# Grouped Ln and Exp in the mixer's front, and weight blocks' lower halves by accumulating DMAs

## The chip, the cores and the metric

The kernel runs on one core of one Trainium2 chip. The metric is the time of one execution in device microseconds (us); the time of the kernel before is the median of three runs. Engines have the profile's names: PE (TensorE's matmuls) and PEld (its weight loads, which overlap them), DVE (VectorE), ACT (ScalarE), POOL (GpSimd) and SP (SyncE, which here only issues DMAs).

## The reference

One decoder layer on 512 tokens of width 1024, with 16 learned tokens put in front (528 rows). After an RMSNorm, one matrix gives all projections. Half of the width goes through RWKV-7 time mixing (8 heads of 64), the other half through an mLSTM (4 heads). Both are joined by `w_out`; then come an RMSNorm and a mixture of 32 SwiGLU experts, of which each token uses two; a last RMSNorm ends it. What the change touches is in the RWKV part:

```python
w_log = -jax.nn.softplus(-(w0 + jnp.tanh(xw @ w_la) @ w_lb)) - 0.5
kk = (k * k_k).reshape(B, L, H, N)
kk = kk / jnp.maximum(jnp.sqrt(jnp.sum(kk * kk, axis=-1, keepdims=True)), 1e-12)
decay = jnp.exp(-jnp.exp(heads(w_log)))
def step(S, inp):
    r_t, d_t, k_t, v_t, a_t, b_t = inp
    Sa = jnp.einsum('bhvk,bhk->bhv', S, a_t)
    S = S * d_t[:, :, None, :] + Sa[..., None] * b_t[:, :, None, :] + v_t[..., None] * k_t[:, :, None, :]
    return S, jnp.einsum('bhvk,bhk->bhv', S, r_t)
y = ((y - mu) * lax.rsqrt(var + LNX_EPS)).reshape(B, L, RWKV_WIDTH)
```

## The kernel before, in words

**Two stages.** The front (projections, RWKV, mLSTM, `w_out`, router) comes first; then the experts, in 16 pairs. A pair's weights are 12 DMAs of 1 MB, so the experts' stage reads some 200 MB. `fetch` (L1731) issues them on SP in order as soon as there is room in SBUF, the first from the planner's mark "var" on (`prefetch`, L1956), most of them when the projections have given their inputs' room back.

**Projections.** `PLAN` (L34) lists 28 blocks of 128 columns: K, R, V for RWKV (four each), v, q, o for the mLSTM, L, M, e, a, b for the low-rank parts. Activations and weights are each split into a rounded upper half and a lower half, and a block is 8 steps (`proj_k`, L600) of (upper, upper), (upper, lower), (lower, upper) on two spans of 264 columns: 48 matmuls, of which the fifth is the first that reads the weights' lower half. `projections` (L1018) prepares the next block after the second step of the current one (L1042) and loads a further one from HBM after the fourth (L1044). `split_block` (L516) makes the halves: ACT casts the raw block to the upper half, and DVE or POOL subtracts that from the raw block. `prepare` (L681) picks the engine: POOL from the mark "P3" to the mark "chain" (and later for q), else DVE. Upper and lower halves have three pairs of places, in the tiles arR and arQ.

**RWKV.** `decays` (L788) makes, per group j of two heads, the decays' running sums and three Exps. `norms` (L826) makes the keys' norms: Square on ACT, a matmul that sums over a head, a max on DVE, then Ln and Exp(-0.5 x) on ACT. `heads` and `products` (L846, L912) make what the 64-token chunks need and set "P0" to "P3". Then `inverse` (L1382) inverts 64 triangular matrices by 31 dependent steps of small DVE operations (`interleaved`, L1345), starting from identity matrices that a DMA of `eye` writes (tile XL, L1386); `inverse0` (L1367) does the same on POOL for the first 16 tokens (XL0, L1374). `chain` (L1490) then walks the chunks, each waiting on the one before. After it `variances` (L1561) makes the heads' variances, per quarter tb: Square, a matmul into one PSUM bank, Ln, and at the end Exp for all four. `outputs_a` (L1584) needs these ("var") and the gate `Gw` of `gate_a` (L1313), and gives what the `mixer` (L1866) multiplies by `w_out`.

**What sets the order.** PE's and SP's instructions run in the order in which they are emitted. `Weave.run` (L422) picks the next generator by rank and by a model of time, `Clock` (L181), in which POOL's `tensor_tensor` costs 2.1 ns per element of a row (L264), a DMA its bytes at 360 GB/s and 2 us more (L244, L290), and a change between Ln and Exp/Tanh 1.28 us (L274). That POOL and DVE hinder each other is not in it. The order on DVE, ACT and POOL is made by the framework's scheduler, from priorities (which follow the order of emission; `tc.high_priority` raises them) and its own estimate of when an instruction's inputs are there. All of the front's instructions are recorded at one line, L308, by a helper.

Of the kernel before, what the change touches and what calls it, by code (L numbers as in the profile page):

```python
# [9 lines left out]
F32 = mybir.dt.float32  # L10
# [7 lines left out]
L = 528  # L18
# [340 lines left out]
class Weave:  # L359
# [21 lines left out]
    def until(self, *names):  # L381
        while any(n not in self.marks for n in names):
            yield self.clock.t + 0.2
# [60 lines left out]
def layer(ctx, tc, a, out, dbg=None, stop=None):  # L444
# [27 lines left out]
    if dbg is not None and "track" in dbg:  # L472
        dbg["track"](A, B)

    def dump(name, ap):
        if dbg is not None and name in dbg:
            Y.dma_start(out=dbg[name], in_=ap)
# [5 lines left out]
    def chunks(t):  # L483

        return t[:, NM:].rearrange("p (c t) -> p c t", t=64)
# [10 lines left out]
    def c(name, i=0, n=1):  # L496
        return cv[:, CV[name][0] + i:CV[name][0] + i + n]
# [9 lines left out]

    lead, rest, small, wide = range(0, 4), range(4, 8), range(4, 6), range(6, 8)


    def load_block(i):
        raw = A.get([128, 1024], name="raw")
        Y.dma_start(out=raw, in_=a["wb"][i])
        return raw

    def split_block(raw, hi_by=S, lo_by=V, among=None):  # L516
        hi, lo = A.get([128, 1024], F32R, "whi", among), A.get([128, 1024], F32R, "wlo", among)
        if hi_by is S:
            S.copy(hi, raw)
        else:  # L520
            gcopy(hi, raw)
        lo_by.tensor_tensor(lo, raw, hi.bitcast(F32), op=OP.subtract)
        A.put(raw)
        return hi, lo, (hi, lo)

# [262 lines left out]
    def decays():  # L788

        yield from until("hwa")  # L790
        for j in range(4):
# [22 lines left out]
            D65 = Dt[:, 17:].rearrange("p (c t) -> p c t", t=65)  # L814
            G.memset(Dt[:, 0:1], 1.0)
            G.memset(D65[:, :, 0:1], 1.0)
            S.activation(Dt[:, 1:17], sg[:, :NM], AF.Exp, scale=-DEC)
            S.activation(D65[:, :, 1:], chunks(sg), AF.Exp, scale=-DEC)
            S.activation(sg, sg, AF.Exp, scale=DEC)
            gcopy(DT[:, j, 0:1], Dt[:, 16:17])  # L820
            gcopy(DT[:, j, 1:9], D65[:, :, 64])
            gates_of[j] = sg, al, Dt, D65
# [2 lines left out]

    def norms():  # L826

        for j in range(4):
            yield from until(f"k{j}")
            yield from W.units(A, 1)  # L830
            sq = A.get([128, L], name="sq")
            S.activation(sq, kx[j], AF.Square, scale=c("k_k", j))
            yield from need(sq)
            pn = yield from bank(2, "pn", rest)
            for h in range(2):
                P.matmul(pn[:, h, :264], m("bones"), sq[:, h * 264:h * 264 + 264], start=True, stop=True)
            V.tensor_scalar(halves(sq), pn[:, :, :264], 1e-24, None, op0=OP.max)
            B.put(pn)
            S.activation(sq, sq, AF.Ln)
            S.activation(sq, sq, AF.Exp, scale=-0.5)  # L840
            V.scalar_tensor_tensor(sq, kx[j], c("k_k", j), sq, op0=OP.mult, op1=OP.mult)
            nks[j] = sq
            yield
            W.mark(f"n{j}")

    def heads():  # L846

# [516 lines left out]
    VS, VU, Wt, SD = [], [], None, None  # L1364
    Btu = Bt.rearrange("p c j x -> p (c j) x")

    def inverse0():  # L1367
        yield from until("P3")
        NC0, NL0 = A.get([128, NM, 32], name="NC0"), A.get([128, NM, 32], name="NL0")
        XL0 = A.get([128, 32, NM], name="XL0")  # L1370
        tm0 = [A.get([128, 64], name="tm0")]
        G.memset(NC0, 0.0)
        gcopy(NC0[:, :, 0:4].rearrange("p t j -> p j t"), Bt0)
        Y.dma_start(out=XL0, in_=a["eye"][None, :, 0:NM].to_broadcast([128, 32, NM]))  # L1374
        V.transpose(NL0.rearrange("p a b -> p (a b)"), NC0.rearrange("p a b -> p (a b)"))
        yield from interleaved(G, XL0, lambda s: NL0[:, s + 1:, s], NM, tm0, 99)
        V.transpose(NC0, XL0.rearrange("p r t -> p t r"))
        gcopy(X0, NC0[:, :, 0:4].rearrange("p t j -> p j t"))
        A.put(NC0, NL0, XL0, *tm0)
        W.mark("X0")  # L1380

    def inverse():  # L1382
        yield from until("P3")
        NL = A.get([128, 32, 32], name="NL")
        XL = A.get([128, 32, 32], name="XL")
        Y.dma_start(out=XL, in_=a["eye"][None].to_broadcast([128, 32, 32]))  # L1386
        tmps = [A.get([128, 256], name="tmp") for _ in range(2)]
        V.transpose(NL.rearrange("p a b -> p (a b)"), NCt.rearrange("p a b -> p (a b)"))
        yield from interleaved(V, XL, lambda s: NL[:, s + 1:, s], 32, tmps, 8)
# [171 lines left out]
    def variances():  # L1561

        f = "p j x -> p (j x)"
        yield from until("chain")
        for tb in range(4):
            W.add(1, variance(tb, yT[tb].rearrange(f), sqs[tb].rearrange(f)))
        yield from until(*(f"var{tb}" for tb in range(4)))
        for sq in sqs:
            S.activation(sq, sq, AF.Exp, scale=-0.5)
        W.mark("var")  # L1570

    def variance(tb, y, sq):
        S.activation(sq, y, AF.Square)
        yield from need(sq)
        pm_ = yield from bank(1, "pm", every)
        P.matmul(pm_, m("bones"), sq, start=True, stop=True)
        S.activation(sq, pm_, AF.Ln, scale=1.0 / 64, bias=m("eps")[:, 1:2])
        yield
        B.put(pm_)
        W.mark(f"var{tb}")  # L1580

    ya = {}

# [379 lines left out]

    W.add(0, heads())
    W.add(0, chain())
    W.add(0.69, inverse0())
    W.add(0, decays())
    W.add(1, norms())
# [378 lines left out]
```

## Time and profile before

| | us |
|---|---|
| median of 3 runs | 905.73 |
| lowest and highest run | 905.42, 906.67 |
| the profiled execution's own time | 904.07 |
| its span, first to last instruction | 902.3 |

| engine | busy us | share |
|---|---|---|
| PE | 826.9 | 92% |
| PEld | 499.0 | 55% |
| DVE | 434.1 | 48% |
| ACT | 264.3 | 29% |
| POOL | 203.1 | 23% |

A share is an average over the whole span. The front and the experts' stage have different limits, so the rows further below are read by stretch. In a row of the timeline, instructions of the same kind that follow each other are merged: its second column is then the time from the first one's start to the last one's end. What stands in square brackets is idle time of the engine ahead of the row, and who ended it.

### The profile page before, as it was taken

To read this page: it belongs to the slowest core of one execution; us is meant where nothing else is said; L and a number is where in the kernel's file an instruction comes from. 1 tells how busy PE (TensorE), PEld (TensorE's weight loads), DVE (VectorE), ACT (ScalarE), POOL (GpSimd) and SP (SyncE) were. 2 spreads that over 40 slices of the span, in tenths; PEclk is the share of its full clock that TensorE was granted. 3 is DMA by queue.
4 is the path that set the end of the run, shared out by engine and by line. 5 is a ranking of instruction groups with operands and counts; after the bars stand their busy time and mean duration, and the time that the engine had idled before them with its cause. 6 is when DMAs were issued, how large, how long until landed. Compare 5 with 4: busy or idle time off the path is not lost. (4 is left out here: it accounts for less than half of the span.)

```text
span 902.3 us, 13658 instructions
## 1 busy us (share of the span) xinstructions
PE 826.9 (92%) x5487; PEld 499.0 (55%) x5488; DVE 434.1 (48%) x819; ACT 264.3 (29%) x505; POOL 203.1 (23%) x278
## 2 busy tenths in 40 slices
PE   7989697878899889999999999999999999999994
PEld 5878596777887767888343444433444423332331
DVE  7677757598746639437132333423333323331324
ACT  5755555634345584312110111001110101001102
POOL 5164625365543328220100000000000000000002
PEclk8988889988998899999999999999999999999998
DMA  6210111311300222989999999999999999999982
GB/s 238 71 42 7 47 63 55 83 34 38 102 25 2 74 84 72 386 329 348 376 406 393 419 420 420 420 420 420 420 420 420 420 421 420 420 419 422 421 349 97
DMA packets 45142, 235.60 MB, mean 261 GB/s; under 512 B 9906, under 2 KB 10290, under 8 KB 21008
## 3 DMA queue, kind: packets, MB, share of 16 engines
q1 hardware_dynamic: 42192, 228.58, 63.6%
q0 software_dynamic: 2160, 3.93, 1.1%
q10 hardware_dynamic: 720, 2.15, 0.6%
q8 instruction: 45, 0.74, 0.3%
q14 instruction: 25, 0.20, 0.1%
HBM read 234.38 MB, written 4.19 MB: 264 GB/s over the span
## 5 line engine op out<-in xcount | busy, mean ns | idle before, releaser
L308 PE MATMUL accs<-arS,arR 128*128 128x264 f32 (+2 forms) x1136 | 180.8, 311 | 8.3 <-DVE arS L308 3.5
L308 PEld LDWEIGHTS accs<-arS,arR 128*128 128x128 f32 (+1 forms) x1136 | 160.6, 199 | 22.4 <-issue 5.5
L308 PE MATMUL accs<-arF 64*64 64x192 f32 (+17 forms) x1361 | 112.6, 289 | 29.8 <-DVE arF L308 20.0
L2072 PE MATMUL accs<-arF 128*64 128x512 f32 x568 | 133.2, 599 | 6.2 <-DMA arF<-wgu 6.1
L2000 DVE TENSOR_TENSOR arF<-arF,accs 128x512 f32<-128x512 f32 x124 | 80.8, 683 | 100.4 <-PE accs L1998 98.9
L308 PEld LDWEIGHTS accs<-arF 64*64 64x64 f32 (+6 forms) x1346 | 83.1, 157 | 46.3 <-DVE arF L308 15.9
L308 POOL TENSOR_TENSOR arF<-arF 128x528 f32<-128x528 f32 (+13 forms) x97 | 89.9, 929 | 83.1 <-DVE arF L308 56.6
L1809 POOL DMA_INDIRECT arM<-hd,arF x15 | 15.1, 1008 | 372.8 <-DVE arF L1799 356.1
L308 DVE TENSOR_TENSOR arF<-arF 64x16 f32<-64x16 f32 (+31 forms) x170 | 90.2, 578 | 7.4 <-POOL arF L308 4.7
L2072 PEld LDWEIGHTS accs<-arF 128*64 128x64 f32 x568 | 37.5, 137 | 87.1 <-issue 65.3
L308 ACT ACTIVATE arF<-arF 128x528 f32<-128x528 f32 (+7 forms) x113 | 59.8, 550 | 74.7 <-DVE arF L308 51.5
L2107 ACT ACTIVATE arF<-accs,arF 128x512 f32<-128x512 f32 x16 | 11.0, 687 | 240.1 <-PE accs L2072 240.1
L308 POOL TENSOR_SCALAR arF<-arF 64x256 f32<-64x256 f32 (+9 forms) x101 | 56.9, 565 | 95.3 <-ACT arF L308 43.2
L2140 DVE SCALAR_TENSOR_TENSOR arO<-accs,arF,arO 128x1024 fp32r<-128x1024 f32 x15 | 19.3, 1284 | 103.2 <-ACT arO L2139 103.2
L2130 PE MATMUL accs<-arF 128*64 128x512 f32 x280 | 63.8, 597 | 0.2 <-DMA arF<-wdn 0.2
L1997 PE MATMUL accs<-arO,OHT 128*128 128x512 f32 x124 | 57.5, 464 | 0.0
L308 ACT COPY arF<-accs 64x256 f32<-64x256 f32 (+7 forms) x111 | 39.8, 370 | 53.8 <-PE accs L308 28.2
L308 DVE TENSOR_TENSOR arF<-accs,arF 128x128 f32<-128x128 f32 (+7 forms) x81 | 35.6, 460 | 29.0 <-PE accs L308 21.1
L1998 PE MATMUL accs<-arO,OHT 128*128 128x512 f32 x124 | 49.0, 395 | 0.0
L308 PE MATMUL accs<-arW,arS 128*128 128x512 f32 x192 | 46.7, 398 | 0.0
L1997 PEld LDWEIGHTS accs<-arO,OHT 128*128 128x128 f32 x124 | 23.3, 188 | 40.4 <-issue 38.1
L2139 ACT ACTIVATE arO<-accs,arF 128x1024 fp32r<-128x1024 f32 x15 | 16.7, 1113 | 98.7 <-PE accs L2130 98.7
(142 smaller groups left out, 930.3 us busy)
## 6 DMA issues: line engine op xcount, KB each, us to landing
arF<-wgu SPq DMA_DIRECT2D x71, 1024.0 KB, 19.8
arF<-wdn SPq DMA_DIRECT2D x35, 1024.0 KB, 19.8
arM<-wgu SPq DMA_DIRECT2D x23, 1024.0 KB, 20.0
arH<-wgu SPq DMA_DIRECT2D x17, 1024.0 KB, 19.8
arN<-wgu SPq DMA_DIRECT2D x16, 1024.0 KB, 18.6
arF<-wb SPq DMA_DIRECT2D x23, 512.0 KB, 3.6
arM<-wdn SPq DMA_DIRECT2D x10, 1024.0 KB, 20.5
arN<-wdn SPq DMA_DIRECT2D x8, 1024.0 KB, 20.4
```

Of the source, the lines that this page charges most:

```text
L308: r = f(*args, **kw)
L1809: nc.gpsimd.indirect_dma_start(out=xt[p % 2], out_offset=None, in_=hd, in_offset=bass.IndirectOffsetOnAxis(ap=idx[:, p % 2:p % 2 + 1], axi ...
L1997: P.matmul(pq, lhs, oh[:, hs], start=True, stop=False)
L1998: P.matmul(pq, lhs, ol[:, hs], start=False, stop=True)
L2000: V.tensor_tensor(hv, hv, pq, op=OP.add)
L2072: P.matmul(pgu[64 * e:64 * e + 64, h], x[:, k, 64 * e:64 * e + 64], w[:, D * e + 512 * h:D * e + 512 * h + 512], start=(k == 0), stop=(k = ...
L2107: S.activation(av, pgu[:, 0], AF.Silu, scale=r1_)
L2130: P.matmul(pdn[64 * e:64 * e + 64, h], aT[:, k, 64 * e:64 * e + 64], w[:, D * h + 512 * e:D * h + 512 * e + 512], start=(k == 0), stop=(k ...
L2139: S.activation(oh, pdf, AF.Copy, scale=g1_)
L2140: V.scalar_tensor_tensor(ol, pdf, g1_, oh.bitcast(F32), op0=OP.mult, op1=OP.subtract)
```

## The change

Four edits. **Lower halves**: where POOL was to subtract, ACT now writes the negated upper half into the lower half's tile, and a DMA on POOL's queue reads the raw block from HBM once more and adds it there. **Identities**: a generator of its own, `identities`, takes the room of XL and XL0 and issues the two `eye` DMAs from the mark "P2" on; `inverse` and `inverse0` wait for its mark. **Norms**: those of j = 0 and 1 are made together, Ln, Ln, Exp, Exp; those of 2 and 3 alone, as before. **Decays and variances**: the decays' three Exps get a higher priority; the variances go into two pairs of PSUM banks, with one Ln per pair, in place, and four Exps that read PSUM, all at a higher priority.

```diff
@@ -472,6 +472,10 @@
+    def sooner(n):
+
+        return tc.high_priority(offset=n)
@@ -507,10 +511,13 @@
+    source = {}
     def load_block(i):
         raw = A.get([128, 1024], name="raw")
         Y.dma_start(out=raw, in_=a["wb"][i])
+        source[id(raw)] = i, raw
         return raw
@@ -519,7 +526,12 @@
-        lo_by.tensor_tensor(lo, raw, hi.bitcast(F32), op=OP.subtract)
+        if lo_by is G:
+
+            S.activation(lo, hi.bitcast(F32), AF.Copy, scale=-1.0)
+            G.dma_start(out=lo, in_=a["wb"][source[id(raw)][0]].rearrange("p k n -> p (k n)"), accum_op=OP.add)
+        else:
+            lo_by.tensor_tensor(lo, raw, hi.bitcast(F32), op=OP.subtract)
@@ -814,9 +826,10 @@
-            S.activation(Dt[:, 1:17], sg[:, :NM], AF.Exp, scale=-DEC)
-            S.activation(D65[:, :, 1:], chunks(sg), AF.Exp, scale=-DEC)
-            S.activation(sg, sg, AF.Exp, scale=DEC)
+            with sooner(200):
+                S.activation(Dt[:, 1:17], sg[:, :NM], AF.Exp, scale=-DEC)
+                S.activation(D65[:, :, 1:], chunks(sg), AF.Exp, scale=-DEC)
+                S.activation(sg, sg, AF.Exp, scale=DEC)
@@ -825,23 +838,26 @@
-        for j in range(4):
-            yield from until(f"k{j}")
...
-            B.put(pn)
-            S.activation(sq, sq, AF.Ln)
-            S.activation(sq, sq, AF.Exp, scale=-0.5)
-            V.scalar_tensor_tensor(sq, kx[j], c("k_k", j), sq, op0=OP.mult, op1=OP.mult)
-            nks[j] = sq
-            yield
-            W.mark(f"n{j}")
+        for js in ((0, 1), (2,), (3,)):
+            for j in js:
+                yield from until(f"k{j}")
...
+                B.put(pn)
+                yield
+            for j in js:
+                S.activation(nks[j], nks[j], AF.Ln)
+            for j in js:
+                S.activation(nks[j], nks[j], AF.Exp, scale=-0.5)
+            for j in js:
+                V.scalar_tensor_tensor(nks[j], kx[j], c("k_k", j), nks[j], op0=OP.mult, op1=OP.mult)
+                W.mark(f"n{j}")
@@ -1364,14 +1380,23 @@
+    eyes = {}
+
+    def identities():
+
+        yield from until("P2")
+        for name, n in (("XL", 32), ("XL0", NM)):
+            eyes[name], = yield from W.room(A, 1, [128, 32, n], F32, name)
+            Y.dma_start(out=eyes[name], in_=a["eye"][None, :, 0:n].to_broadcast([128, 32, n]))
+        W.mark("eyes")
+
     def inverse0():
-        yield from until("P3")
+        yield from until("P3", "eyes")
...
-        Y.dma_start(out=XL0, in_=a["eye"][None, :, 0:NM].to_broadcast([128, 32, NM]))
...
     def inverse():
-        yield from until("P3")
+        yield from until("P3", "eyes")
...
-        Y.dma_start(out=XL, in_=a["eye"][None].to_broadcast([128, 32, 32]))
+        XL = eyes["XL"]
@@ -1562,22 +1586,24 @@
-        for tb in range(4):
-            W.add(1, variance(tb, yT[tb].rearrange(f), sqs[tb].rearrange(f)))
-        yield from until(*(f"var{tb}" for tb in range(4)))
-        for sq in sqs:
-            S.activation(sq, sq, AF.Exp, scale=-0.5)
+        for sq, y in zip(sqs, yT):
+            S.activation(sq.rearrange(f), y.rearrange(f), AF.Square)
+        pms = []
+        for i in range(2):
+            pm = yield from bank(2, "pm", every)
+            pms.append(pm)
+            for h in range(2):
+                sq = sqs[2 * i + h].rearrange(f)
+                yield from need(sq)
+                P.matmul(pm[:, h], m("bones"), sq, start=True, stop=True)
+            yield
+        with sooner(200):
+            for pm in pms:
+                S.activation(pm, pm, AF.Ln, scale=1.0 / 64, bias=m("eps")[:, 1:2])
+            for tb, sq in enumerate(sqs):
+                S.activation(sq.rearrange(f), pms[tb // 2][:, tb % 2], AF.Exp, scale=-0.5)
+        B.put(*pms)
         W.mark("var")
...
@@ -1963,6 +1989,7 @@
     W.add(0, chain())
+    W.add(0, identities())
```

## Rows read from the trace of the kernel before

**Rows 1.** The page's span in 40 equal slices: granted PE clock in tenths

```profile
PEclk8988889988998899999999999999999999999998
```

**Rows 2.** Stretches: length, busy PE, PEld, DVE, ACT, POOL; granted clock, DMA share, GB/s

```profile
0.00:355.00 355.00, 303.93 (x2833) 265.20 (x2835) 244.94 (x420) 189.60 (x369) 166.21 (x230) 0.90 0.21 66
355.00:430.00 75.00, 74.39 (x423) 61.79 (x423) 39.20 (x126) 20.49 (x55) 16.44 (x21) 1.00 0.85 328
430.00:886.00 456.00, 445.27 (x2222) 169.81 (x2218) 143.08 (x264) 49.90 (x70) 15.99 (x17) 1.00 0.99 407
```

**Rows 3.** Timeline of PE in the front: start, us, what, idle ahead and its end

```profile
181.40 7.58 PE L308 MATMUL accs<-arS,arR 128*128 128x264 f32 x60
193.19 2.62 PE L308 MATMUL accs<-arF 128*128 128x128 f32 x10 [4.21 <-DVE arF L308]
195.74 3.78 PE L308 MATMUL accs<-arS,arR 128*128 128x264 f32 x18
...
213.49 1.98 PE L308 MATMUL accs<-arS,arR 128*128 128x264 f32 x14 [0.73 <-POOL arR L308]
218.87 3.80 PE L308 MATMUL accs<-arF 32*32 32x32 f32 x128 [3.41 <-DVE arF L308]
222.61 4.71 PE L308 MATMUL accs<-arS,arR 128*128 128x264 f32 x24
...
237.03 0.62 PE L308 MATMUL accs<-arF 64*16 64x64 f32 x16 [2.11 <-ACT arF L308]
...
334.00 0.49 PE L308 MATMUL accs<-arW 128*128 128x512 f32 x1 [2.92 <-ACT arW L308]
```

**Rows 4.** POOL's groups by shape, 170 to 236 us: count, busy us, mean ns, idle before

```profile
L308 POOL TENSOR_TENSOR arR<-arF,arR 128x1024 fp32r<-128x1024 f32 x6 | 15.3, 2551 | 4.6 <-ACT arR L308 4.5
```

**Rows 5.** Timeline of DVE in the inverse and behind it

```profile
179.76 0.32 DVE L308 TENSOR_TENSOR arF<-arF 128x156 f32<-128x156 f32 x1
180.65 2.42 DVE L308 TENSOR_TENSOR arF<-arF 128x175 f32<-128x175 f32 x1
211.22 2.37 DVE L308 TENSOR_TENSOR arF<-arF 128x78 f32<-128x78 f32 x1
233.55 2.59 DVE L308 TENSOR_TENSOR arF<-arF 128x256 f32<-128x256 f32 x1
```

**Rows 6.** Timeline of ACT and DVE after the chain

```profile
316.57 1.28 ACT L308 ACT_TABLE_LOAD   x1
...
328.06 1.28 ACT L308 ACT_TABLE_LOAD   x1
328.07 0.69 DVE L308 TENSOR_TENSOR arW<-arF,arW 128x512 fp32r<-128x512 f32 x1 [4.42 <-ACT arW L308]
```

**Rows 7.** Timeline of ACT at the norms of j = 0 and 1

```profile
38.09 1.28 ACT L308 ACT_TABLE_LOAD   x1
...
47.35 0.64 ACT L308 ACTIVATE arF<-arF 64x528 f32<-64x528 f32 x1
```

**Rows 8.** Timeline of ACT: three casts of an upper half, 128x1024

```profile
178.90 1.05 ACT L308 CAST arR<-arF 128x1024 fp32r<-128x1024 f32 x1
198.35 1.05 ACT L308 CAST arR<-arF 128x1024 fp32r<-128x1024 f32 x1 [1.09 <-PE accs L308]
205.68 1.05 ACT L308 CAST arR<-arF 128x1024 fp32r<-128x1024 f32 x1 [3.69 <-POOL arF L308]
```

**Rows 9.** DMA issues (count, KB each, median us to landing) and POOL's issuing instruction

```profile
arF<-wb SPq DMA_DIRECT2D x23, 512.0 KB, 3.6
...
arM<-hd,arF POOLq DMA_INDIRECT x15, 8.5
L1809 POOL DMA_INDIRECT arM<-hd,arF x15 | 15.1, 1008 | 372.8 <-DVE arF L1799 356.1
```

**Rows 10.** Timelines of SP and DVE at the inverse's start

```profile
169.89 0.82 SPq L308 DMA_DIRECT2D arF<-eye  x2
175.31 0.78 DVE L308 TENSOR_TENSOR arF<-arF 128x31 f32<-128x31 f32 x3
```

More of the change, by code (lines that the diff above doesn't have):

```diff
@@ L826, in norms @@
     def norms():
-        for j in range(4):
-            yield from until(f"k{j}")
[L830 to L837, printed above, removed]
-            B.put(pn)
-            S.activation(sq, sq, AF.Ln)
-            S.activation(sq, sq, AF.Exp, scale=-0.5)
-            V.scalar_tensor_tensor(sq, kx[j], c("k_k", j), sq, op0=OP.mult, op1=OP.mult)
-            nks[j] = sq
-            yield
-            W.mark(f"n{j}")
+        for js in ((0, 1), (2,), (3,)):
+            for j in js:
+                yield from until(f"k{j}")
+                yield from W.units(A, 1)
+                sq = nks[j] = A.get([128, L], name="sq")
+                S.activation(sq, kx[j], AF.Square, scale=c("k_k", j))
+                yield from need(sq)
+                pn = yield from bank(2, "pn", rest)
+                for h in range(2):
+                    P.matmul(pn[:, h, :264], m("bones"), sq[:, h * 264:h * 264 + 264], start=True, stop=True)
+                V.tensor_scalar(halves(sq), pn[:, :, :264], 1e-24, None, op0=OP.max)
+                B.put(pn)
[7 more added lines that the diff above has]
+                W.mark(f"n{j}")
     def heads():
@@ L1365, in layer @@
     Btu = Bt.rearrange("p c j x -> p (c j) x")
+    eyes = {}
[5 more added lines that the diff above has]
+        W.mark("eyes")
     def inverse0():
-        yield from until("P3")
+        yield from until("P3", "eyes")
         NC0, NL0 = A.get([128, NM, 32], name="NC0"), A.get([128, NM, 32], name="NL0")
-        XL0 = A.get([128, 32, NM], name="XL0")
+        XL0 = eyes["XL0"]
         tm0 = [A.get([128, 64], name="tm0")]
@@ L1382, in inverse @@
     def inverse():
-        yield from until("P3")
+        yield from until("P3", "eyes")
         NL = A.get([128, 32, 32], name="NL")
-        XL = A.get([128, 32, 32], name="XL")
-        Y.dma_start(out=XL, in_=a["eye"][None].to_broadcast([128, 32, 32]))
+        XL = eyes["XL"]
         tmps = [A.get([128, 256], name="tmp") for _ in range(2)]
@@ L1564, in variances @@
         yield from until("chain")
-        for tb in range(4):
-            W.add(1, variance(tb, yT[tb].rearrange(f), sqs[tb].rearrange(f)))
-        yield from until(*(f"var{tb}" for tb in range(4)))
-        for sq in sqs:
-            S.activation(sq, sq, AF.Exp, scale=-0.5)
-        W.mark("var")
[L1572 to L1580, printed above, removed]
+        for sq, y in zip(sqs, yT):
[4 more added lines that the diff above has]
+            pms.append(pm)
+            for h in range(2):
+                sq = sqs[2 * i + h].rearrange(f)
+                yield from need(sq)
+                P.matmul(pm[:, h], m("bones"), sq, start=True, stop=True)
[6 more added lines that the diff above has]
+        B.put(*pms)
+        W.mark("var")
     ya = {}
```

## The prediction

> **What bounds the kernel now.** I read the busy time by stretch first. In the experts' stage the DMA share is 0.99, so that stage lasts as long as its weights take to arrive [rows 2]. In the joint ahead of it PE is busy for 74.39 of 75 us. In the front it is busy for 303.93 of 355 us, at a granted clock of 0.90, and DMA at a share of 0.21. So the time is the front's length plus a fixed stage: the expert weights are fetched into room that the projections give back, so what the front loses at its end is lost by everything behind it, one for one. The question is what becomes of the 51 us in which PE idles.
>
> PE's timeline says who ends these waits [rows 3]. From the inverse on they are 4.21 us on DVE, 0.73 on POOL's lower half, 3.41 on DVE, 2.11 on ACT and, after the chain, 2.92 on ACT: 13.4 us in sum. PE takes its instructions in a fixed order, so nothing fills such a hole.
>
> What makes DVE late is seen beside POOL. POOL's six lower halves take 2551 ns each [rows 4]. During each of the four that fall into the inverse, the one DVE operation then in flight takes 2.4 us, where its neighbour of nearly the same shape takes 0.32; the first and the last of the four stand in [rows 5]. DVE is held for as long as POOL reads its two inputs. That is some 2.1 us each, 8.4 us in a chain of 31 dependent steps. The sixth holds an operation of 128x256 for 2.59 us, close ahead of the copies for which PE waits at 237.03.
>
> The holes cost more than their length. Behind the wait of 4.21 us, 18 matmuls take 3.78 us, and behind that of 3.41 us, 24 take 4.71; ahead of them 60 of the same take 7.58 [rows 3]. That is 210 and 196 ns each instead of 126, in slices where the granted clock falls below its upper level of 2.4 GHz [rows 1], and it costs 1.5 and 1.7 us.
>
> **The change, part by part.**
>
> *Lower halves.* Removed: six subtractions on POOL, hence the 8.4 us on DVE and some 2 us behind the inverse. I take the waits of 4.21, 0.73 and 3.41 us as gone and the one of 2.11 too, and with them the 3.2 us of slow matmuls: 13.7 us. Bounds: none of it if the waits only move, all of it at most.
>
> Added: six negations on ACT, each like the cast of the same size, 1.05 us [rows 8]; ACT is busy for only 189.60 of 355 us [rows 2], so they count only inside a lower half's own path. And six DMAs on POOL's queue. Each waits there for ACT's negation, and behind it in POOL's order stand the small steps of `inverse0` and the copies of `values`; the former's result is first read in the chain, behind the wait at 237.03, so they can spare a few us.
>
> Now the path: cast 1.05, negation 1.05, issue 1.01 (POOL's only DMA instruction so far [rows 9]), then the landing, x. For x the trace has two neighbours: a plain load of the same 512 KB from SP, 3.6 us, and the gathers of 512 KB on POOL's queue, 8.5, taken while the experts' weights fill the DMA engines [rows 9]. The DMA engines are as idle in this stretch as for the plain loads, but an adding DMA must also read what it adds to; I take 5 and keep both ends. The skill has a figure: by DMA: Bandwidth & Descriptors, section "Anatomy of one DMA — SWDGE (gpsimd) path", such a DMA takes 2.0 us plus its bytes at 436 GB/s, here 3.2 us by my estimate, with nothing said of adding; the Trainium skill would thus make the stalls below vanish, and no run here shows it yet.
>
> When is the lower half due? The fifth matmul of a block reads it. A block of 48 begins 24 matmuls into the run of 60 at 181.40, so at 184.4, and the cast for it began at 178.90: 6.0 us [rows 3, 8]. The cast at 198.35 is followed by the next block's at 205.68, which begins as PE lets go of a block, so it has some 7.9 us; the one at 205.68 is due when PE waited, at 212.76 (213.49 less 0.73): 7.1 us [rows 3, 8]. The other three have ten or more. With a path of 3.1 + x, PE stalls x - 2.9, x - 4.8 and x - 4.0 us: at 5 that is 3.3 us, at 3.6 it is 0.7, at 8.5 it is 13.8. I add 1.5 us for one slow stretch behind the longest stall: 4.8 us.
>
> *Variances.* Between 316.57 and 328.06 ACT loads a table six times at 1.28 us [rows 6], because the scheduler has put each Exp where it was ready, between the Ln. With one Ln per pair and raised priority I expect two loads, so 5.1 us less. What hangs on it: DVE waits 4.42 us for a cast that stands behind these loads, and behind DVE comes the low-rank gate for which PE waits 2.92 us at 334.00 [rows 3, 6]. That wait goes; the rest of the 5.1 is slack, since PE has projections to do. Four banks held for a few us instead of one at a time cost nothing as long as the projections, which use one or two, find the other four; a wait for a bank would be at most a block's length, some 6 us by 48 matmuls of 126 ns.
>
> Here the Trainium skill speaks against the edit. ScalarE: Activation LUTs, section "Table sets: the hidden batching unit", says that one set holds both exp and ln, so that ln followed by exp needs one load. If this program's loads followed it, grouping would be worth nothing and the sum would be less by 2.92 us. The rows have a load at each change, so I go by them.
>
> *Norms.* Of four loads from 38.09 on two go, 2.6 us. The tanh at 47.35, which starts the decays, could come up to 1.8 us sooner [rows 7]. PE has projections to multiply meanwhile; I cost it at 0 and bound it by 0 and -2.6 us. Without that cover the decays would carry it all.
>
> *Decays' priority* and *identities*: the Exps have nothing dear ahead of them. The `eye` DMAs are issued at 169.89, and the first DVE step comes at 175.31 [rows 10], later than a load of 3.6 us takes [rows 9]; nothing waits for them now, so 0. They take SBUF earlier, and on SP they come ahead of weight blocks; if one had to wait for its place, blocks behind it would be late. Bound: 0 to 4 us.
>
> **Sum**: -13.7 + 4.8 - 2.9 = -11.8 us. The profiled execution took 904.07 us, so 892.3 by its clock; the median is 1.66 us above it, and I say 894.
>
> **Rivals.** *The plan moves* (0.17). PE's order comes from a model that puts a POOL subtraction at 2.1 ns x 1024 and the DMA at its bytes and 2 us, so the lower halves come later in the plan and the matmuls are laid out anew. For: 51 - 13 us of PE's idle time belongs to places that this change doesn't touch, so a new order can make new holes. Against: the plan never knew that POOL holds DVE, so it comes closer to the chip now. If two thirds of the gain come back as other holes, 902.
>
> *Ln and Exp stay mixed* (0.10): the second pair's Ln isn't ready when the first pair's Exps are, and the scheduler takes them first, as it does now. Then 334.00 keeps its 2.92 us, and it is 897. This is the case in which the change doesn't do what it says.
>
> *The adding DMA lands late* (0.11), slower. At x = 8.5 the three blocks stall for 13.8 us, three slow stretches behind them cost some 1.6 us each, and one more block becomes late by 1 to 2: 20 us against a gain of 16.6 in all, so 909. It decides from x of about 8 on. Against it: DMA is nearly idle in this stretch; for it: 8.5 is the only landing on this queue in the trace.
>
> **Numbers.** My forecast has 0.62. The lower end takes the shortest landing, the norms' bound and a faster stretch after 334.00: -20 us, 884. The upper end reaches over the moved plan to 904; what lies above is the late DMA and part of the moved plan. A measurement can tell 0.2%, 1.8 us, from no change. Faster: 0.62 + 0.10 + 0.10 of the moved plan = 0.82; same 0.07; slower 0.11.
>
> **What would show it.** Right: no POOL operation of 128x1024 on arR between 170 and 236 us, no DVE step of the inverse above 0.8 us, the inverse some 8 us shorter; waits like those at 193.19 and 218.87 gone; two table loads after the chain; PE's idle time in the front about 40 us. The landing of the six DMAs is read from the DMA issues: near 5 us, with waits of PE on a DMA into arR of about 3 us in sum. Wrong: landings near 8 us or more, or waits of PE of several us at new places in the front.

## The result and the profile after

The changed kernel takes 893.43 us, median of four runs (891.54 to 896.87), beside 905.58 for the kernel before (904.56 to 906.67): 0.9892 of it, 95% interval 0.9866 to 0.9919. 894.0 was forecast, with 884 to 904. The profiled execution took 891.54 us, with a span of 889.8 (before: 904.07 and 902.3).

The changed kernel's granted clock on the page, as in [rows 1]:

```profile
PEclk8998999996998999999999999999999999999998
```

Its busy time by stretch (columns as in [rows 2]):

```profile
0.00:345.00 345.00, 298.54 (x2843) 258.34 (x2845) 233.96 (x420) 194.24 (x373) 157.70 (x231) 0.93 0.28 78
345.00:420.00 75.00, 73.71 (x422) 60.45 (x422) 39.60 (x125) 19.23 (x53) 15.96 (x21) 1.00 0.87 339
420.00:874.00 454.00, 443.32 (x2217) 169.39 (x2213) 143.12 (x265) 50.33 (x70) 15.87 (x17) 1.00 0.99 407
```

The front's granted clock is 0.93, where it was 0.90: of its 16 slices four are below 9, where nine were, though one of the four, from 200 us on, is at 6. The joint and the experts' stage are as long as before. The gain is the front's: the projections' last matmul ends at 345.72 us, where it ended at 357.97. That is 12.2 us, and the span is 12.5 us shorter, so what the front won came out at the end one for one.

The same columns from the start to that end, the kernel before first:

```profile
0.00:357.97 357.97, 306.90 (x2847) 267.58 (x2849) 247.91 (x423) 192.32 (x373) 168.40 (x231) 0.90 0.21 65
0.00:345.72 345.72, 299.26 (x2847) 258.88 (x2849) 234.68 (x420) 194.24 (x373) 158.42 (x231) 0.93 0.28 79
```

PE does the same 2847 matmuls in both. So the 12.2 us are two things: PE idles 46.5 us in place of 51.1, which is 4.6, and its matmuls are busy for 7.6 us less, at the higher granted clock.

PE's timeline in the front after the change, cut to the longer waits (columns as in [rows 3]):

```profile
68.43 1.93 PE L308 MATMUL accs<-arF 64*64 64x192 f32 x14 [3.64 <-DVE arF L308]
...
151.45 2.60 PE L308 MATMUL accs<-arF 64*64 64x192 f32 x32 [3.61 <-DVE arF L308]
...
184.99 4.04 PE L308 MATMUL accs<-arS,arR 128*128 128x264 f32 x20 [3.25 <-DMA arR<-wb]
189.78 1.48 PE L308 MATMUL accs<-arF 128*128 128x128 f32 x10 [0.74 <-DVE arF L308]
...
202.97 3.82 PE L308 MATMUL accs<-arF 32*32 32x32 f32 x128 [2.03 <-DVE arF L308]
...
325.46 4.00 PE L308 MATMUL accs<-arW 128*128 128x512 f32 x16 [1.29 <-ACT arF L308]
```

The waits of 4.21 and 3.41 us on DVE [rows 3] have become 0.74 and 2.03, and one wait on an adding DMA has come, 3.25 us. But two waits of 3.6 us have come at 68 and 151 us, where the kernel before had 4.18 at 94 and 3.21 at 113: PE's order differs from early on, well ahead of the first lower half in question.

The only group of POOL's that now writes arR, with the columns of [rows 4]:

```profile
L308 POOL DMA_DIRECT2D arR<-wb x7 | 6.4, 919 | 2.3 <-ACT arR L308 2.1 <-ACT arF L308 0.2
```

The adding DMAs in the list of DMA issues (count, KB each, median us to landing):

```profile
arR<-wb POOLq DMA_DIRECT2D x7, 512.0 KB, 6.2
```

The timeline of DVE at the longer of the first steps of the inverse:

```profile
169.76 1.27 DVE L308 TENSOR_TENSOR arF<-arF 128x135 f32<-128x135 f32 x1
```

And POOL's at that moment:

```profile
169.33 1.54 POOL L308 TENSOR_TENSOR arF<-arF 128x512 f32<-128x512 f32 x1
```

DVE's transposes, between which the inverse lies, in the kernel before:

```profile
173.34 1.25 DVE L308 STREAM_TRANSPOSE arF<-arF 128x1024 f32<-128x1024 f32 x1 [0.61 <-ACT arF L308]
...
217.57 3.03 DVE L308 STREAM_TRANSPOSE arF<-arF 128x1024 f32<-128x1024 f32 x2
```

The operation of [rows 4] is gone; seven adding DMAs (not six) stand in its place. No step of the inverse is held for 2.4 us any more [rows 5]; two are held for some 1.3 us by other POOL work. From DVE's transpose to transpose the inverse takes 38.3 us in place of 44.2, and it also starts 10 us sooner (163.36 against 173.34); ahead of it PE does 1045 matmuls in place of 1101.

ACT at the variances, after the change:

```profile
297.77 1.28 ACT L308 ACT_TABLE_LOAD   x1
299.06 1.09 ACT L308 ACTIVATE accs<-accs,arF 128x1024 f32<-128x1024 f32 x1
300.17 1.28 ACT L308 ACT_TABLE_LOAD   x1
301.46 1.09 ACT L308 ACTIVATE arF<-accs 128x512 f32<-128x512 f32 x2
302.57 1.28 ACT L308 ACT_TABLE_LOAD   x1
303.86 1.09 ACT L308 ACTIVATE accs<-accs,arF 128x1024 f32<-128x1024 f32 x1
...
305.50 1.28 ACT L308 ACT_TABLE_LOAD   x1
```

Four loads, not two: the second pair's Ln was not ready when the first pair's Exps were. At the norms of j = 0 and 1 there are four loads as before (37.89, 40.45, 42.40 and 44.36). So the grouping happened only in part, and three questions were open: what the lower halves are worth, what the new order of PE is worth, and whether the ACT edits gave anything through their table loads.

### The profile page after: what moved, and what is told of

It is laid out like the page before. It is cut to its first block, busy times and chain, and to the rows that moved or that the text cites. A ratio compares the mean times of both kernels' runs of the same rounds, so it can differ in the third digit from the quotient of the medians.

```text
span 889.8 us, 13684 instructions
## 1 busy us (share of the span) xinstructions
PE 818.8 (92%) x5487; PEld 490.3 (55%) x5488; DVE 423.5 (48%) x818; ACT 267.7 (30%) x508; POOL 194.0 (22%) x279
## 3 DMA queue, kind: packets, MB, share of 16 engines
q1 hardware_dynamic: 42192, 228.58, 64.5%
## 5 line engine op out<-in xcount | busy, mean ns | idle before, releaser
L308 PE MATMUL accs<-arS,arR 128*128 128x264 f32 (+2 forms) x1120 | 178.5, 307 | 11.7 <-DMA arR<-wb 3.2
L308 PEld LDWEIGHTS accs<-arS,arR 128*128 128x128 f32 (+1 forms) x1120 | 155.6, 194 | 26.2 <-DVE arS L308 4.6
L308 PE MATMUL accs<-arF 64*64 64x192 f32 (+17 forms) x1361 | 110.5, 285 | 30.6 <-DVE arF L308 21.0
L308 PEld LDWEIGHTS accs<-arF 64*64 64x64 f32 (+8 forms) x1346 | 80.3, 155 | 48.3 <-ACT arF L308 17.9
L308 DVE TENSOR_TENSOR arF<-arF 64x16 f32<-64x16 f32 (+31 forms) x170 | 79.9, 519 | 10.3 <-POOL arF L308 5.7
L308 ACT ACTIVATE arF<-arF 128x528 f32<-128x528 f32 (+6 forms) x109 | 57.6, 549 | 89.4 <-DVE arF L308 58.0
L308 POOL TENSOR_SCALAR arF<-arF 64x256 f32<-64x256 f32 (+9 forms) x101 | 54.8, 544 | 79.8 <-ACT arF L308 43.6
L308 ACT COPY arF<-accs 64x256 f32<-64x256 f32 (+7 forms) x111 | 39.9, 370 | 42.4 <-PE accs L308 18.9
L308 DVE TENSOR_TENSOR arF<-accs,arF 128x528 f32<-128x528 f32 (+7 forms) x81 | 35.6, 460 | 25.6 <-PE accs L308 18.6
```

Of the source, the lines that this page charges most:

```text
L308: r = f(*args, **kw)
```

## The experiments

All were timed with the kernel before beside them. Several keep PE's order in the front fixed by telling the planner of other work than is done; the comparison with the kernel whose order they keep is then one of the chip, not of plans.

| run | us | before beside it | ratio (95%) |
|---|---|---|---|
| adding DMAs alone | 906.00 | 904.69 | 1.0032 (1.0006 to 1.0058) |
| all but the adding DMAs | 905.81 | 904.69 | 1.0030 (1.0013 to 1.0048) |
| adding DMAs in the old order of PE | 900.72 | 904.69 | 0.9959 (0.9939 to 0.9979) |
| POOL reads one input, old order | 897.87 | 904.69 | 0.9919 (0.9887 to 0.9950) |
| changed kernel again | 894.90 | 904.37 | 0.9887 (0.9851 to 0.9922) |
| POOL subtracts in the new order | 900.67 | 904.37 | 0.9972 (0.9949 to 0.9995) |
| changed, grouping made good | 892.74 | 904.37 | 0.9880 (0.9845 to 0.9914) |
| adding DMAs and norms | 899.56 | 904.37 | 0.9949 (0.9927 to 0.9970) |
| changed without identities | 894.93 | 903.42 | 0.9894 (0.9871 to 0.9917) |
| DVE subtracts in the new order | 900.62 | 903.42 | 0.9966 (0.9953 to 0.9979) |
| grouping and split lower halves | 893.57 | 903.42 | 0.9891 (0.9866 to 0.9915) |
| adding DMAs and variances | 897.49 | 903.42 | 0.9940 (0.9908 to 0.9971) |

### Each half of the change alone

The kernel before with the lower halves' edit alone:

```diff
+        source[id(raw)] = i, raw
...
-        lo_by.tensor_tensor(lo, raw, hi.bitcast(F32), op=OP.subtract)
+        if lo_by is G:
+            S.activation(lo, hi.bitcast(F32), AF.Copy, scale=-1.0)
+            G.dma_start(out=lo, in_=a["wb"][...], accum_op=OP.add)
```

> The kernel before with the adding DMAs alone (ACT negates, a DMA on POOL's queue adds; norms, decays, identities and variances as before). Theory A, the lower halves carry the gain because POOL's two-input operation held DVE: most of the prediction's 13.7 us less what PE waits for late halves. With the landing of 6.2 us that the changed kernel shows, the three stalls are 3.3, 1.4 and 2.2 us and one slow stretch 1.5, so 5 us faster, at most 9: 897 to 901. The inverse (44.2 us from DVE's transpose to transpose) becomes 6 to 8 us shorter. Rival B, the gain comes from a new order of PE that the other edits bring about (in the changed kernel the inverse starts 10 us sooner): 904 to 907 here, with the waits only moved.

And the changed kernel with that edit taken back:

```diff
-            S.activation(lo, hi.bitcast(F32), AF.Copy, scale=-1.0)
-            G.dma_start(out=lo, in_=a["wb"][...], accum_op=OP.add)
+            G.tensor_tensor(lo, raw, hi.bitcast(F32), op=OP.subtract)
```

> The changed kernel with POOL's subtraction put back, so norms, decays, identities and variances alone. Theory A: little, 902 to 905 (up to 2.9 us by the variances, which load four tables instead of six and not two), DVE held again for 2.4 us at four or five steps of the inverse, and waits of PE on DVE of 3 to 4 us around the inverse. Rival B: 894 to 897, since the inverse starts some 10 us sooner here too and that is what counts.

Neither half gives anything: 906.00 and 905.81 us, both a little above the kernel before. Theory A missed the first and theory B the second. Yet both mechanisms are there: in the first the inverse takes 38.0 us in place of 44.2, in the second it starts at 163.31. In the first PE idles 49.4 us up to the projections' end, against 51.1 before (its profiled execution, of 902.86 us, was its shortest). A part of what the shorter inverse gave is lost again behind the chain. Its timeline of PE:

```profile
349.07 6.92 PE L308 MATMUL accs<-arS,arR 128*128 128x512 f32 x22 [4.34 <-DVE arR L308]
```

Its timeline of DVE ahead of that:

```profile
338.24 8.56 DVE L308 TENSOR_TENSOR arF<-arF 128x512 f32<-128x512 f32 x5
346.73 2.29 DVE L308 TENSOR_TENSOR arR<-arF,arR 128x1024 fp32r<-128x1024 f32 x1
348.94 1.28 DVE L308 TENSOR_TENSOR arF<-arF 128x512 f32<-128x512 f32 x2
```

And POOL's:

```profile
342.84 1.75 POOL L308 TENSOR_TENSOR arW<-arF,arW 128x512 fp32r<-128x512 f32 x1
344.55 3.38 POOL L308 TENSOR_TENSOR arF<-arF 128x512 f32<-128x512 f32 x2
```

The same matmuls in the kernel before:

```profile
352.61 5.36 PE L308 MATMUL accs<-arS,arR 128*128 128x512 f32 x22 [1.66 <-DVE arR L308]
```

PE waits 4.34 us, where it waited 1.66, for a lower half that DVE makes behind five operations of 1.71 us each (8.56 in all); two of the same size take 1.28 us at 348.94. POOL runs two-input operations of 1.7 us through that stretch. So DVE and POOL hinder each other behind the chain as well, where the change does nothing about it, and how much of that PE feels depends on its order there.

### The lower halves with PE's order held fixed

First the adding DMAs in the order of the kernel before:

```diff
+            nc.scalar.activation(lo, hi.bitcast(F32), AF.Copy, scale=-1.0)
+            nc.gpsimd.dma_start(out=lo, in_=a["wb"][...], accum_op=OP.add)
+            clock.tell("G", "tensor_tensor", (lo, raw, hi.bitcast(F32)), dict(op=OP.subtract))
```

> As the run with the adding DMAs alone, but the planner is told POOL's old subtraction in place of the negation and the DMA, so that PE's order in the front stays that of the kernel before, matmul by matmul. Theory A: what POOL and the DMA do to the chip is the cause, not the plan: the inverse 6 to 8 us shorter, the waits of 4.21 and 3.41 us on DVE gone or below 1 us, and in their place waits on a DMA of up to 7 us in sum; 896 to 901. Rival B: without a new order no gain, 904 to 907.

900.72 us, as theory A had it: 5.3 us below the same work in its own order (906.00). The inverse takes 35.5 us in place of 44.2. This run's profiled execution was its longest, 907.77 us, so only places and waits are read from it. DVE's transposes:

```profile
175.08 1.25 DVE L308 STREAM_TRANSPOSE arF<-arF 128x1024 f32<-128x1024 f32 x1 [0.60 <-ACT arF L308]
...
210.58 3.10 DVE L308 STREAM_TRANSPOSE arF<-arF 128x1024 f32<-128x1024 f32 x2
```

PE's timeline:

```profile
189.72 5.70 PE L308 MATMUL accs<-arS,arR 128*128 128x264 f32 x32 [2.93 <-DMA arR<-wb]
...
209.48 2.39 PE L308 MATMUL accs<-arS,arR 128*128 128x264 f32 x14 [3.16 <-DMA arR<-wb]
...
241.49 3.45 PE L308 MATMUL accs<-arS,arR 128*128 128x264 f32 x14 [2.46 <-DMA arR<-wb]
```

The waits of 4.21, 0.73 and 3.41 us [rows 3] are gone, and three waits on adding DMAs, 8.5 us in sum where up to 7 were expected, stand in their place. They take back most of what the waits on DVE gave: PE idles 48.3 us up to the projections' end, against 51.1.

Then POOL's operation made shorter, with no DMA in it:

```diff
+        if lo_by is G:
+            nc.gpsimd.tensor_scalar(lo, raw, 2.0 ** -12, 0.0, op0=OP.mult, op1=OP.add)
+            clock.tell("G", "tensor_tensor", (lo, raw, hi.bitcast(F32)), dict(op=OP.subtract))
```

> The kernel before with POOL's subtraction of 128x1024 replaced by a scaling of the raw block, which reads one input; the planner is told the old cost, and PE's order stays. It leaves the subtraction out, so the lower half is not one. Theory A, POOL's reading of two inputs holds DVE: no DVE step of the inverse longer than 1 us beside these operations, the inverse 7 to 9 us shorter, the four waits of 10.5 us gone with their slow matmuls, no wait on a DMA: 892 to 896, so more than the adding DMAs give alone. Rival C, DVE is held by any POOL operation of this size: DVE steps of 1.3 to 2 us beside them, 899 to 903. Rival B: 904 to 907.

897.87 us, between theory A and rival C. One step of the inverse in the timeline of DVE:

```profile
179.70 1.15 DVE L308 TENSOR_TENSOR arF<-arF 128x135 f32<-128x135 f32 x1
```

And POOL's operation at that moment:

```profile
179.53 1.05 POOL L523 TENSOR_SCALAR arR<-arF 128x1024 fp32r<-128x1024 f32 x1
```

So reading one input holds DVE too, for as long as the operation lasts: 1.15 us for a POOL operation of 1.05, as 2.42 [rows 5] for one of 2.67 before. The inverse takes 38.7 us. The prediction's "reads its two inputs" was too narrow. The Trainium skill, SBUF — State Buffer, section "Who interferes with whom", says that a DVE instruction with two SBUF inputs contends with any GpSimd instruction that reads SBUF; this run agrees with it. The halved hold alone, without a wait on a DMA, is worth 0.8%: PE idles 42.4 us, against 51.1.

Last, POOL's subtraction in the order of the changed kernel, beside the changed kernel itself:

```diff
+            nc.gpsimd.tensor_tensor(lo, raw, hi.bitcast(F32), op=OP.subtract)
+            clock.tell("S", "activation", (lo, hi.bitcast(F32), AF.Copy), dict(scale=-1.0))
+            clock.tell("G", "dma_start", (), dict(out=lo, in_=a["wb"][...], accum_op=OP.add))
```

> The changed kernel with POOL's subtraction in place of the negation and the adding DMA, while the planner is still told of the negation and the DMA: PE's order in the front is that of the changed kernel, and only POOL, ACT and the DMAs differ. The adding DMAs alone gave nothing in their own new order of PE and 4 us in the order of before; the other edits alone gave nothing. Theory D, the lower halves carry the gain, but only where PE's order lets it through: the inverse is 6 to 8 us longer here than in the changed kernel and 900 to 906 comes out. Rival B, the new order of PE by itself, with whatever makes the lower halves: 893 to 897.

The changed kernel, with no edit:

> The changed kernel once more, as the base for the runs beside it: 892 to 896, 0.987 to 0.992 of the kernel before.

894.90 against 900.67 us: theory D. PE's timeline with POOL's subtraction:

```profile
195.28 2.62 PE L308 MATMUL accs<-arF 128*128 128x128 f32 x10 [8.24 <-DVE arF L308]
197.83 6.28 PE L308 MATMUL accs<-arS,arR 128*128 128x264 f32 x36
...
212.71 5.42 PE L308 MATMUL accs<-arF 32*32 32x32 f32 x192 [2.38 <-DVE arF L308]
```

The same matmuls in the changed kernel, second run:

```profile
190.05 4.14 PE L308 MATMUL accs<-arS,arR 128*128 128x264 f32 x20 [3.04 <-DMA arR<-wb]
193.99 1.50 PE L308 MATMUL accs<-arF 128*128 128x128 f32 x10
195.42 4.64 PE L308 MATMUL accs<-arS,arR 128*128 128x264 f32 x36
...
205.65 3.80 PE L308 MATMUL accs<-arF 32*32 32x32 f32 x128 [0.49 <-DVE arF L308]
```

A wait of 8.24 us on a DVE that is held becomes one of 3.04 on a DMA, and the wait of 2.38 becomes 0.49: 7.1 us. The matmuls behind the longer wait also take longer, 2.62 against 1.50 us for ten and 6.28 against 4.64 for 36. Over the whole front, though, the gain is in the waits: up to the projections' end PE idles 52.9 us with POOL's subtraction and 44.2 with the adding DMAs, while its matmuls are busy for 300.4 and 304.1. With the adding DMAs taken out, the new order and the other edits' work together give 0.9972, some 3.7 us.

### DVE instead, and a faster landing

If DVE need only not be held, it could subtract itself, in half the time that it was held for:

```diff
+            nc.vector.tensor_tensor(lo, raw, hi.bitcast(F32), op=OP.subtract)
+            clock.tell("S", "activation", (lo, hi.bitcast(F32), AF.Copy), dict(scale=-1.0))
+            clock.tell("G", "dma_start", (), dict(out=lo, in_=a["wb"][...], accum_op=OP.add))
```

> The changed kernel with the subtraction on DVE in place of ACT's negation and the adding DMA; the planner is told of the negation and the DMA, so PE's order stays. A subtraction of this size takes DVE 1.22 us, about half of what it was held for. Theory A: the inverse gets some 5 us of subtractions between its steps (43 us in place of 38), the wait of 3.0 us on a DMA goes, and PE's waits on DVE grow by 2 to 5 us: 893 to 898, close to the changed kernel and faster than POOL's subtraction in the same order (900.7). Rival: what matters is that DVE is kept free at all, 898 to 902.

900.62 us, as with POOL's subtraction: the rival. PE's timeline:

```profile
188.91 1.83 PE L308 MATMUL accs<-arF 128*128 128x128 f32 x10 [4.39 <-DVE arF L308]
...
208.16 3.82 PE L308 MATMUL accs<-arF 32*32 32x32 f32 x128 [6.63 <-DVE arF L308]
```

The inverse takes 42.8 us, as expected, but PE's waits on DVE are 11.0 us here, where the changed kernel has 3.0 on a DMA and 0.5 on DVE. In this stretch the inverse is what PE waits for, and the five subtractions of 1.2 us each that DVE now does between its steps come out in the time.

The split of the lower half, on top of the grouping below:

```diff
+            for h in (slice(0, 512), slice(512, 1024)):
+                nc.scalar.activation(lo[:, h], hi[:, h].bitcast(F32), AF.Copy, scale=-1.0)
+            for h in range(2):
+                nc.gpsimd.dma_start(out=lo[:, h * 512:h * 512 + 512], in_=a["wb"][...], accum_op=OP.add)
```

> The changed kernel with the grouping of Ln and Exp made good, and each lower half made in two parts of 512 columns: two negations, two adding DMAs of 256 KB, the part that PE reads first ahead. PE's order stays. The one wait of 3.0 us on a DMA shrinks if the first part lands sooner: by the negation's half, 0.5 us, and whatever a DMA of half the bytes saves, so to between 0.5 and 2.5 us: 890 to 893. If the landing is a fixed time whatever the bytes, or the second issue (0.9 us on POOL) is in the way of POOL's steps, 892 to 895 as without it.

PE's timeline:

```profile
187.64 2.69 PE L308 MATMUL accs<-arS,arR 128*128 128x264 f32 x20 [1.33 <-DMA arR<-wb]
192.25 0.94 PE L308 MATMUL accs<-arF 128*128 128x128 f32 x6 [1.92 <-DVE arF L308]
```

The DMA issues:

```profile
arR<-wb POOLq DMA_DIRECT2D x14, 256.0 KB, 5.5
```

The wait shrinks from 3.04 to 1.33 us, and the 20 matmuls behind it take 2.69 in place of 4.14. But at once DVE is late in its place, by 1.92 us where there was no wait, and the time (0.9891) is that of the changed kernel. Half the bytes land only 0.3 us sooner by the medians: 5.5 us, against 5.8 in the run below that has the same grouping and whole DMAs.

### The ACT edits

The grouping made good:

```diff
             for j in js:
-                S.activation(nks[j], nks[j], AF.Ln)
-            for j in js:
-                S.activation(nks[j], nks[j], AF.Exp, scale=-0.5)
+                last = S.activation(nks[j], nks[j], AF.Ln)
+            with tc.issue_after(last.ins):
+                for j in js:
+                    S.activation(nks[j], nks[j], AF.Exp, scale=-0.5)
```

and the same at the variances' Exps.

> The changed kernel with the grouping made good: each Exp of the norms' pair and of the variances is put behind the last Ln by an edge of order on ACT alone, so that the norms' pair and the variances take two table loads each instead of four; PE's order stays. By the prediction's prices the variances' wait of 1.29 us of PE at 324 goes and the norms give 0 to 2.6 us: 1 to 4 us below the changed kernel. Rival E, both lie under PE's projections and the norms' tanh hardly moves: within 1 us of the changed kernel. An Exp that now waits for a later Ln could also be late: up to 2 us above.

0.9880 beside 0.9887: no difference that these runs can tell. The timeline of ACT at the tanh behind the norms and at the variances' second load:

```profile
47.25 0.65 ACT L308 ACTIVATE arF<-arF 64x528 f32<-64x528 f32 x1 [1.84 <-POOL arF L308]
...
302.07 1.28 ACT L308 ACT_TABLE_LOAD   x1
```

And that of PE at the wait that the prediction put down to the loads:

```profile
325.15 3.99 PE L308 MATMUL accs<-arW 128*128 128x512 f32 x16 [1.37 <-ACT arF L308]
```

Both groups now have two loads (at 37.80 and 42.00, and at 298.67 and 302.07). The tanh at 47 us does not come sooner, since it waits for POOL, and PE's wait at 325 is still 1.37 us: it did not hang on the loads.

Adding DMAs with the norms' and decays' edits only: the changed kernel with the variances and the identities as they were before.

```diff
-        for sq, y in zip(sqs, yT):
-            S.activation(sq.rearrange(f), y.rearrange(f), AF.Square)
...
+        for tb in range(4):
+            W.add(1, variance(tb, yT[tb].rearrange(f), sqs[tb].rearrange(f)))
...
-        XL = eyes["XL"]
+        XL = A.get([128, 32, 32], name="XL")
+        Y.dma_start(out=XL, in_=a["eye"][None].to_broadcast([128, 32, 32]))
```

> The kernel before with the adding DMAs, the norms and the decays' priority; variances and identities as before. PE's order is that of the changed kernel up to the chain's end. Theory F, what lets the gain of the lower halves through is the order that the norms' edit brings about ahead of the inverse, which starts some 7 us sooner than with the adding DMAs alone: 893 to 898. Theory G, it is what comes behind the chain (the variances): 902 to 907, with the chain's end near 290 us and the projections' end near 355 all the same.

899.56 us, between the theories: 0.8% below the adding DMAs alone, 0.6% above the changed kernel. PE behind the chain:

```profile
314.01 1.25 PE L308 MATMUL accs<-arS,arR 128*128 128x264 f32 x4 [7.25 <-ACT arF L308]
```

ACT meanwhile:

```profile
307.24 1.28 ACT L308 ACT_TABLE_LOAD   x1
308.53 0.63 ACT L308 ACTIVATE arF<-arF 128x512 f32<-128x512 f32 x1
...
311.98 1.28 ACT L308 ACT_TABLE_LOAD   x1
313.27 0.69 ACT L308 ACTIVATE arF<-accs,arF 128x512 f32<-128x512 f32 x1
```

PE waits 7.25 us, until the Ln of the last quarter, which reads `accs`, ends at 313.96. The matmuls behind the wait read arS and arR and write `accs`, so what they wait for must be the PSUM bank that this Ln gives back. And that Ln stands behind two table loads, an Exp that was taken first, and other work on ACT.

The changed kernel without the identities, so with norms and variances:

```diff
-    W.add(0, identities())
...
-        XL = eyes["XL"]
+        XL = A.get([128, 32, 32], name="XL")
+        Y.dma_start(out=XL, in_=a["eye"][None].to_broadcast([128, 32, 32]))
```

> The changed kernel without the identities' edit; PE's order stays the changed kernel's throughout the front. With the variances and the norms in, without the identities. If the identities are worth nothing, as the prediction has it, 893 to 897 as the changed kernel, and the wait of 7.25 us for a bank near 307, which the run with adding DMAs and norms alone showed, is gone: then the variances' edit is what took it away. If the identities carry a part, 898 to 901.

894.93 us, 0.9894: the identities are worth nothing that these runs can tell. PE's timeline where the wait of 7.25 us was:

```profile
306.04 0.76 PE L308 MATMUL accs<-arS,arR 128*128 128x264 f32 x4 [0.28 <-DVE arF L308]
```

So the variances' edit took it away. Beside the norms it is worth 0.9949 - 0.9894, 5 us; PE's order behind the chain differs between these two runs, so this is the edit's work and its order together.

Last, adding DMAs and variances: as the run before, but with the norms and the decays of the kernel before.

```diff
-        for js in ((0, 1), (2,), (3,)):
-            for j in js:
+        for j in range(4):
...
-            with sooner(200):
```

> The kernel before with the adding DMAs and the variances' edit, norms, decays and identities as before; PE's order up to the chain's end is that of the run with the adding DMAs alone (906.0). If the parts add, the variances take 4 to 5 us off that, as they do beside the norms: 900 to 903. If the variances pay only behind the order that the norms' edit brings about, 904 to 907.

897.49 us, below the range of either theory. The variances take 0.9% off the adding DMAs alone, so they pay without the norms' order too. The norms' and decays' edits then take another 0.46% off, 4 us, though the norms' table loads stayed at four. This second figure is loose: five of the twelve runs lie between 891.3 and 893.6, as fast as the changed kernel, five between 902.1 and 903.5, and the two intervals (0.9908 to 0.9971, 0.9871 to 0.9917) overlap.

## Why the prediction was right

The number was right (893.43 for 894.0), and so was its first cause; its terms were not all right, and those that were wrong went both ways. That the sum came out within 1 us is in part luck.

**The bound** held: the front's 12.2 us are the span's 12.5.

**The lower halves** held in mechanism, and in the size that could be checked apart: the inverse was to become 8.4 us shorter, and with PE's order held fixed it became 8.7 shorter (44.2 to 35.5). So did the slow matmuls: 1.5 us were put behind the longest stall, and the 20 matmuls behind the wait on the DMA take 4.14 us against 2.69 behind the short one. What was mis-sized is x, the landing: 5 us were taken, 6.2 measured in the changed kernel's first profile and 5.5 to 5.9 in the later ones with whole DMAs. (The Trainium skill's rule from DMA: Bandwidth & Descriptors, section "Anatomy of one DMA — SWDGE (gpsimd) path", had given 3.2 by my estimate; the measurement stands.) The three stalls x - 2.9, x - 4.8 and x - 4.0 are at 6.2 then 6.9 us instead of 3.3, and the term is -13.7 + 6.9 + 1.5 = -5.3 instead of -8.9. The run in the old order (x = 5.8, so 5.7 us of stalls) had three such waits, of 8.5 us in sum, the third at 241 us at a block that had been given ten us or more, and gained 4.0 us by the medians. In the new order there is only one such wait, and the edit is worth 5.8 us (894.90 against 900.67).

**The variances** were priced at -2.9 us, by way of two loads instead of six and PE's wait at 334.00 [rows 3, 6]. The step "that wait goes" failed: with four loads it is 1.29 us, with two 1.37. Beside the norms the edit is worth about 5 us all the same, for another reason: the six loads also held up the Ln that gives a PSUM bank back, and in that order PE waits for that bank. The prediction looked at banks only as a cost of the edit. The bank is not the whole account: beside the adding DMAs alone the edit took off more (906.00 to 897.49, the latter a loose median), though there PE's longest wait on ACT behind the inverse is 2.0 us; what it gave in that order stays open. The Trainium skill's rule from ScalarE: Activation LUTs, section "Table sets: the hidden batching unit", which spoke against the edit, is not what this program shows: it still loads at each change between Ln and Exp, 18 loads in all. By that rule the edit was worth nothing. With the grouping made good, the saved loads were worth nothing that the runs can tell, but the edit was worth something.

**The norms** were priced at 0, with -2.6 at most. For their loads that was right: with two loads the tanh is no sooner. But the edit moved PE's order: the inverse starts 4 to 8 us sooner than without it (between 163 and 167 us in the runs that have it, at 170 and 171 with the adding DMAs alone and with the variances), and the time is some 4 us less, as loosely as said above. That was no term of the sum.

**The identities** at 0 were right. The decays' priority was never tried by itself.

**The rivals.** *Ln and Exp stay mixed* came true, at the norms in full and at the variances in part, without the 2.9 us that it was to cost. *The plan moves* came true as well, and both ways: the adding DMAs in the order that the planner made for them alone take 5.3 us more than in the old order, which took the gain back; with the other edits in the plan, the new order and those edits' work are together worth 3.7 us. The rival had been given only one sign. *The adding DMA lands late* did not come.

**The signs.** POOL's operation is gone, the inverse is shorter, and the waits at 193.19 and 218.87 have shrunk to 0.74 and 2.03 us. But two steps of the inverse take 1.3 us, above 0.8; there are four table loads behind the chain, not two; PE's idle time is 46.5 us, not about 40; and waits of 3.6 us at 68 and 151 us are of the kind that was to show the forecast wrong. These cost little: ahead of the inverse PE idles 29.5 us, against 27.7 before.

**The sum.** 11.8 us stand against 9.5 to 12.2 measured: in the runs made side by side 9.5, which are 5.8 for the lower halves and 3.7 for the order with the other edits. What is in it is not what was forecast. Up to the projections' end, with the same 2847 matmuls each, in one profiled execution of each run:

| run | end us | PE busy | PE idle | granted clock |
|---|---|---|---|---|
| before | 357.97 | 306.9 | 51.1 | 0.90 |
| changed kernel | 345.72 | 299.3 | 46.5 | 0.93 |
| changed kernel again | 348.38 | 304.1 | 44.2 | 0.92 |
| POOL subtracts in the new order | 353.29 | 300.4 | 52.9 | 0.92 |

The forecast took 10.1 us off PE's waits (10.5 and 2.9, less 3.3) and 1.7 off slow matmuls. The waits fell by 4.6 and 6.8 us in the two executions, and the matmuls' time by 7.6 and 2.8: faster matmuls, which the sum nearly left out, made up for waits that stayed, in the first more than in the second. The lower halves' part (last two rows) is waits, 8.7 us, with 3.7 lost again in the matmuls' time. The other part (first and last row) holds no gain in waits: there PE idles 1.8 us longer and is busy for 6.5 less.

What stays open is why one order takes 5 us more than another for the same work: each run shows where its waits lie, but no run tells which of the planner's choices puts them there, or what makes the matmuls faster in one order. The granted clock alone does not order the runs: two of one order, the changed kernel's second run and the one without identities, have 0.965 and 0.958 over the whole span, which is 894.9 and 894.2 us.

## What to carry to other kernels

When a planner lays out an engine's order from modelled costs, every edit is two changes, to the work and to the order; hold the order fixed (tell the planner the old cost) before you believe a part's price, and do not add up parts that were measured alone. An engine that is off the critical path can hold one that is on it, as POOL's operations on SBUF held DVE's: look for instructions whose duration equals that of a neighbour on the other engine. And a table load on ACT can cost PE a PSUM bank: ask not only who reads the result of what stands behind the load, but what it gives back.

## What the runs showed of the hardware that was not expected

An adding DMA is dear for its bytes. With seven of them the queue's packets take 3.7% of 16 engines' span in place of 1.1%, for 3.67 MB more: some 10 GB/s per engine (3.67 MB over 2.6% of 16 times 890 us), where the plain loads' queue moves 228.58 MB in 64.5%, 25 GB/s. It lands after 5.5 to 6.2 us (medians of the runs) where a plain load of the same 512 KB takes 3.6 [rows 9], and after 5.5 us with half the bytes.

DVE and POOL slow each other both ways: back to back, DVE's operations of 128x512 took 1.71 us instead of 0.64, and POOL's of that size 1.7, where in the same run the one at 333.26, ahead of that stretch and beside a single DVE operation, took 1.30.
